# Two passes over half of the tokens, and Strassen's seven block products for gate and up

## The chip, the core and the metric

The program runs on one core of a Trainium2 chip. TensorE multiplies and writes PSUM; VectorE (DVE), ScalarE (ACT) and GpSimd (POOL) do the elementwise work; SyncE (SP) issues the DMAs. PEld is TensorE's weight load. The metric is the device time of one execution in microseconds (us). Before the change three runs took 1820.6, 1825.97 and 1830.25 us; the median is 1825.97.

## The reference

One layer of a decoder: input projection, sparse attention beside a state-space layer, output projection, then a feed-forward network (FFN). The change touches the FFN on 1024 prompt tokens and 32 sample tokens, with D_MODEL 1024 and D_FF 2816:

```python
x = x + gate1 * mix
h = rmsnorm(x, prm['norm_ffn_g']) * (1.0 + scale2) + shift2
f = (jax.nn.silu(h @ prm['w_ffn_gate']) * (h @ prm['w_ffn_up'])) @ prm['w_ffn_down']
return x + gate2 * f
```

All is float32. The kernel multiplies in TensorE's fp32r type: each operand is split into a high part (a cast on ACT) and a low part (a subtraction), and a product is three matmuls: high with high, high with low, low with high.

## The kernel before

The mix phase multiplies tiles of 128 tokens by the output projection (`mix_product`, tiles mx6, mx5, ...), adds the residual, and normalizes (`mix_norm`, tiles mn6, ...: eight transposes, then a modulation that leaves the token tile transposed and split in `h2h` and `h2l`, 1056 columns for 1024 prompt and 32 sample tokens). A string, `REST`, gives the order in which the program is written: `x6` is the product of tile 6, `n6` its norm, `f2` a third of the FFN's first step.

The FFN walks D_FF in 22 steps f of 128 columns. A step loads 512 KB each of gate, up and down weights, splits them (L409 cast on ACT, L410 subtraction on DVE), and multiplies gate and up with all tokens in three thirds of 352 columns (L1810: 2 weights x 8 row blocks x 3 matmuls a third, 144 a step). Silu (L1813), the product (L1816) and the split of the result (L1817 on ACT, L1818 on POOL) follow. Every second step, `down` multiplies two steps' results by the down weights: 8 token tiles x 2 halves x 6 matmuls of 512 columns (L1853, 96 a pair of steps), each group of six added to `acc` in SBUF by DVE (L1859). After the last step acc is scaled on POOL (L1843), the residual is added (L1844), and the last groups go out (L1862 to L1864).

A scheduler orders the instructions of each engine when the program is built, by estimates of their times; each engine then runs its own list in order. Tiles have a fixed number of buffers (`bufs`); a new tile waits until the one whose buffer it takes has been read.

Of the kernel before, what the change touches and what calls it, by code (L numbers as in the profile page):

```python
# [89 lines left out]
class Kernel:  # L90
# [1573 lines left out]
    def phase_mix(self):  # L1664
        for tt in self.MIX:
            self.mix_product(tt)
        h2 = self.open("h2", side="right")
        self.h2h = h2.tile([128, 8, 1056], F32R, name="h2h")
        self.h2l = h2.tile([128, 8, 1056], F32R, name="h2l")
        self.pw = self.open("pw", side="right")  # L1670
# [71 lines left out]
    def mix_norm(self, tt, xn):  # L1742
# [6 lines left out]
        if tt < 8:  # L1749
            self.modulated(xn, self.h2h[:, :, sl], self.h2l[:, :, sl], 2, 3, wo, nm, "xn", 2, self.ps_s(nm + "t"))  # L1750
        else:
            h = wo.tile([128, 8, 128], F32, tag="xn", name="h2s").rearrange("p k n -> p (k n)")[:, :256].rearrange("p (k n) -> p k n", k=8)
# [4 lines left out]

    def phase_ffn(self, first):
# [4 lines left out]
        acc = pe.tile([128, 8, 1024], F32, name="acc", bufs=1)  # L1763
        accs = pe.tile([128, 512], F32, name="accs", bufs=1)
        pend = []
        for f in range(NF):
            if f:
                first = self.ffn_weights(f, pe)
                for n in (2, 0, 1):
                    self.ffn_gate(f, n, *first)  # L1770
                first = first[1:]
            ah, al, as_ = first
            dn = pe.tile([128, 1024], F32, tag="wd", name=f"wd{f}", bufs=3)
            nc.sync.dma_start(dn, A["w_ffn_down"][0, 128 * f:128 * f + 128])
            dh = pe.tile([128, 1024], F32R, tag="dh", name=f"dh{f}")
            dl = pe.tile([128, 1024], F32R, tag="dl", name=f"dl{f}")
            self.split(dn, dh, dl)
            pend.append((dn, dh, dl, ah, al, as_))
            if len(pend) == 2:
                self.down(f, pend, acc, accs, pe)  # L1780
                pend = []
        self.close("pe", "pf", "pw", "h2", "pse")

    def ffn_weights(self, f, pe):

        nc, A, pf = self.nc, self.A, self.pf
        W = []
        for i, n in enumerate(("w_ffn_gate", "w_ffn_up")):
            raw = self.pw.tile([128, 8, 128], F32, tag="wr", name=f"wr{f}_{i}", bufs=2)
            nc.sync.dma_start(raw, A[n][0].rearrange("(k p) n -> p k n", p=128)[:, :, 128 * f:128 * f + 128])  # L1790
            wh, wl = ((pe if f % 2 else pf).tile([128, 8, 128], F32R, tag=f"w{f % 2}", name=f"w{x}{f}_{i}", bufs=4) for x in "hl")
            self.split(raw, wh, wl)
            W.append((wh, wl))
        ah, al = ((pe if f % 3 else pf).tile([128, 1024], F32R, tag="ahl", name=f"a{x}{f}", bufs=4 if f % 3 else 2) for x in "hl")
# [111 lines left out]
```

## Time and profile before

| | us |
|---|---|
| median of three runs | 1825.97 |
| lowest, highest | 1820.6, 1830.25 |
| the profiled execution | 1828.84 |
| its span, first to last instruction | 1827.1 |
| PE busy (94%) | 1709.1 |
| DVE busy (53%) | 972.2 |
| ACT busy (34%) | 618.9 |
| POOL busy (23%) | 427.1 |

The profile's time of one matmul runs from its start to its modelled end, and matmuls overlap, so the cost of one in a stream is the distance from one start to the next in the timeline. Busy shares of a stage come from a view by windows.

### The profile page before, as it was taken

The numbers are of one execution on the slowest core, as the hardware profiler recorded it, in microseconds if no ns is written. First come the engines' busy times: TensorE is split into PE (matmuls) and PEld (weight loads), VectorE is DVE, ScalarE is ACT, GpSimd is POOL, SyncE is SP. The second block draws the span as 40 slices with busy tenths as digits, with TensorE's granted clock in tenths as the row PEclk, the third lists the DMA queues.
The fourth block names the chain that finished last, engine by engine and source line by source line (L and its number), as shares of the span: only waits on it lengthen the run. The fifth ranks groups of instructions, "written<-read, shape, count | busy, mean of one in ns | idle before, by whom it ended". The sixth has DMA issues, their size and how long they took to land.

```text
span 1827.1 us, 29355 instructions
## 1 busy us (share of the span) xinstructions
PE 1709.1 (94%) x11546; PEld 1439.4 (79%) x11546; DVE 972.2 (53%) x2330; ACT 618.9 (34%) x1247; POOL 427.1 (23%) x817
## 2 busy tenths in 40 slices
PE   6998999899796899999989989999999999999997
PEld 3898988788564665655657888998998999999996
DVE  4867647588988466566535443323333333333346
ACT  4523146455453355565433341111111111211210
POOL 2344545232015313341122210110110110110150
PEclk9999999899898999999999999999999999999999
DMA  8333243645231345413114221101201201201113
GB/s 297 105 86 106 70 152 119 219 157 193 65 112 63 71 161 195 152 61 104 55 60 138 92 93 58 58 24 50 67 24 47 70 24 47 70 24 47 53 47 141
DMA packets 132699, 172.43 MB, mean 94 GB/s; under 512 B 17176, under 2 KB 92312, under 8 KB 132304
## 3 DMA queue, kind: packets, MB, share of 16 engines
q1 hardware_dynamic: 123024, 136.62, 23.4%
q0 software_dynamic: 9408, 33.89, 5.8%
q8 instruction: 91, 1.49, 0.3%
q14 instruction: 48, 0.39, 0.1%
q10 hardware_dynamic: 128, 0.04, 0.0%
HBM read 143.88 MB, written 25.46 MB: 93 GB/s over the span
## 4 chain that ended last, share of the span: by engine, by line
PE 61%; DVE 6%; DMA 4%; ACT 2%; issue 1%; POOL 1%; SPq 1%; DVEq 0%; ACTq 0%; POOLq 0%
PE gu L1810 19%; PE dn L1853 13%; PE g L1810 5%; PE u L1810 4%; PE aso L1283 3%; PE as L1205 1%; PE as L1206 1%; SPq L1596 1%; PE acs L1258 1%; PE mx8M L1728 1%; PE mx2M L1728 1%; PE mx5M L1728 1%; PE mx0M L1728 1%; PE mx1M L1728 1%; PE mx4M L1728 1%
## 5 line engine op out<-in xcount | busy, mean ns | idle before, releaser
L1810 PE MATMUL gu<-h2h,wh 128*128 128x352 f32 x704 | 227.8, 324 | 5.0 <-ACT h2h L870 5.0
L1810 PE MATMUL gu<-h2h,wl 128*128 128x352 f32 x704 | 227.3, 323 | 0.0
L1810 PE MATMUL gu<-h2l,wh 128*128 128x352 f32 x704 | 226.8, 322 | 0.0
L1859 DVE TENSOR_TENSOR acc<-acc,dn 128x512 f32<-128x512 f32 x144 | 98.9, 687 | 229.9 <-PE dn L1853 229.9
L1818 POOL TENSOR_TENSOR al<-fa,ah 128x352 fp32r<-128x352 f32 (+1 forms) x66 | 69.6, 1054 | 414.8 <-ACT ah L1817 408.8
L1813 ACT ACTIVATE fa<-gu 128x352 f32<-128x352 f32 x44 | 20.4, 465 | 412.1 <-PE gu L1810 412.1
L1853 PE MATMUL dn<-dh,ah 128*128 128x512 f32 x352 | 140.3, 399 | 5.6 <-DVE fin L1862 5.2
L1810 PEld LDWEIGHTS gu<-h2h,wh 128*128 128x128 f32 x704 | 132.5, 188 | 7.9 <-ACT h2h L870 5.3
L1853 PE MATMUL dn<-dl,ah 128*128 128x512 f32 x352 | 138.7, 394 | 0.0
L1853 PE MATMUL dn<-dh,al 128*128 128x512 f32 x352 | 138.3, 393 | 0.0
L1810 PEld LDWEIGHTS gu<-h2l,wh 128*128 128x128 f32 x704 | 133.0, 189 | 3.8
L1810 PEld LDWEIGHTS gu<-h2h,wl 128*128 128x128 f32 x704 | 132.7, 188 | 3.1
L1816 DVE TENSOR_TENSOR fa<-fa,gu 128x352 f32<-128x352 f32 x44 | 22.9, 521 | 143.0 <-ACT fa L1813 143.0
L409 ACT CAST wh<-wr 128x1024 fp32r<-128x1024 f32 x44 | 46.0, 1048 | 151.8 <-PE g L1810 77.0
L1205 PE MATMUL as<-kst,aqA 128*128 128x320 f32 (+4 forms) x192 | 76.7, 403 | 16.2 <-ACT ap L1222 9.3
L1853 PEld LDWEIGHTS dn<-dh,ah 128*128 128x128 f32 x352 | 66.1, 188 | 24.5 <-ACT wh L409 7.5
L410 DVE TENSOR_TENSOR wl<-wr,wh 128x1024 fp32r<-128x1024 f32 x44 | 58.8, 1339 | 49.3 <-ACT wh L409 49.3
L1853 PEld LDWEIGHTS dn<-dl,ah 128*128 128x128 f32 x352 | 66.1, 188 | 15.6
L1853 PEld LDWEIGHTS dn<-dh,al 128*128 128x128 f32 x352 | 66.3, 188 | 8.1
L1222 ACT ACTIVATE ap<-as,asm 128x640 f32<-128x640 f32 (+3 forms) x64 | 55.8, 873 | 46.6 <-DVE asm L1221 31.3
L1221 DVE TENSOR_REDUCE asm<-as 128x1 f32<-128x640 f32 (+3 forms) x64 | 58.5, 918 | 20.7 <-PE as L1209 19.8
L1206 PE MATMUL as<-kst,aqB 128*128 128x320 f32 (+4 forms) x192 | 65.1, 344 | 4.7 <-ACT aqB L1168 4.7
(2137 smaller groups left out, 4667.9 us busy)
## 6 DMA issues: line engine op xcount, KB each, us to landing
wada<-in_w_ada SPq DMA_DIRECT2D x24, 1024.0 KB
wr<-in_w_ffn_gate SPq DMA_DIRECT2D x22, 512.0 KB
wr<-in_w_ffn_up SPq DMA_DIRECT2D x22, 512.0 KB
wd<-in_w_ffn_down SPq DMA_DIRECT2D x22, 512.0 KB
bx<-in_x_prompt SPq DMA_DIRECT2D x8, 512.0 KB
s_raw<-in_cache_kv_win SPq DMA_DIRECT2D x8, 512.0 KB
wor<-in_w_out SPq DMA_DIRECT2D x16, 256.0 KB
ex<-x_d SPq DMA_DIRECT2D x8, 512.0 KB
```

Source lines behind the costliest of these rows:

```text
L409: self.nc.scalar.copy(hi, raw)
L410: self.nc.vector.tensor_tensor(lo, raw, hi.bitcast(F32), op=ALU.subtract)
L1205: nc.tensor.matmul(Sv, qA[:, h, :], kk, start=True, stop=False)
L1206: nc.tensor.matmul(Sv, qB[:, h, :], kk, start=False, stop=not mt)
L1221: nc.vector.tensor_reduce(mx[:, :1], Sv, axis=ax, op=ALU.max, negate=True)
L1222: nc.scalar.activation(Pv, Sv, AF.Exp, bias=mx[:, :1], accum_out=l[:, h:h + 1])
L1283: nc.tensor.matmul(O[64 * g:64 * g + 64, 256 * hf:256 * hf + 256], V[:n, 64 * g:64 * g + 64], pT[:, 256 * g:256 * g + 256], start=first, s ...
L1728: nc.tensor.matmul(M[:P, :], X[k][b], w[:, k, c], start=m == 0, stop=m == 23)
L1810: nc.tensor.matmul(gu[i], w[:, k, :], h[:, k, 352 * n:352 * n + 352], start=m == 0, stop=m == 23)
L1818: nc.gpsimd.tensor_tensor(al[:, cols], a[:, :w], ah[:, cols].bitcast(F32), op=ALU.subtract)
L1853: nc.tensor.matmul(p, a[:, sl], w[:, c], start=m == 0, stop=m == 5)
L1859: nc.vector.tensor_tensor(o, o, p, op=ALU.add)
```

## The change

The block matrix with gate and up as one axis and the two halves of the 1024 rows of h as the other is multiplied with a 2 x 2 arrangement of the activations (row half by token half). Instead of eight block products a step there are seven, of sums of blocks ("forms"), numbered 1, 5, 6, 2, 7, 4, 3 in the order in which they are written. For that the tokens are cut in two passes of 528 columns (PASS), each pass in two halves of 264. Each pass walks all 22 steps, so every weight is loaded, summed and split twice. A product is 4 row blocks x 3 matmuls of 264 columns; X, Z and Y are PSUM accumulators, and X is copied out three times on the way (fa), while the next product goes on adding to it. The seven forms of the activations (F1 to F7) are built once a pass: for the first in the mix phase (`F` in REST), for the second from a copy in DRAM (`h_d`, tiles hb). The FFN's first step no longer stands between the mix products.

```diff
@@ -1664,27 +1664,33 @@
     def phase_mix(self):
         for tt in self.MIX:
             self.mix_product(tt)
...
+        self.fm = self.open("fm", side="right")
+        self.h_d = self.scratch("h_d", (128, 16 * 264)).rearrange("p (a b k n) -> p a b k n", a=2, b=2, k=4)
+        self.hr = self.open("hr")
+        self.raw = self.hr.tile([128, 2, 2, 4, 264], F32, name="hraw")
         self.tags = "tt"
...
+            elif kind == "F":
+                self.ffn_forms(0, self.raw, self.hr)
+                self.close("hr")
+                self.pw = self.open("pw", side="right")
+                self.pf = self.open("pf", side="right")
+                self.hs = self.pf.tile([128, NF, 32], F32, name="hs")
+                first = self.ffn_weights(0)
...
-    REST = "x6 n8 x5 n7 x0 n6 x1 n5 n0 f2 n1 x4 x2 n2 x3 n4 f0 n3 f1"
+    PASS = ((7, 6, 0, 1), (5, 4, 2, 3))
+    REST = "x6 n8 x0 n7 x1 n6 n0 n1 F x5 x4 n5 n4 x2 n2 x3 n3"
...
+            for half in range(2):
+                for kh in range(2):
+                    nc.vector.tensor_copy(self.raw[:, kh, half, :, 256:], h[:, 4 * kh:4 * kh + 4, 8 * half:8 * half + 8])
+                    nc.sync.dma_start(self.h_d[:, kh, half, :, 256:], h[:, 4 * kh:4 * kh + 4, 16 + 8 * half:24 + 8 * half])
...
+        if ps:
+            for kh in range(2):
+                nc.sync.dma_start(self.h_d[:, kh, half, :, c], h[:, kh])
     def phase_ffn(self, first):
@@ -1760,119 +1785,187 @@
...
+        for ps in range(2):
+            acc = pe.tile([128, 4, 1024], F32, tag="acc", name=f"acc{ps}", bufs=1)
+            pend = []
+            if ps:
+                B = self.pe_blocks(pe)
+                self.ffn_forms(1, B, pe)
+            for f in range(NF):
+                if ps or f:
+                    first = self.ffn_gate(ps, f, self.ffn_weights2(self.ffn_weights(f), pe), pe)
+                ah, al = first
+                dn = pe.tile([128, 1024], F32, tag="wd", name=f"wd{ps}{f}")
+                nc.sync.dma_start(dn, A["w_ffn_down"][0, 128 * f:128 * f + 128])
+                dh = pe.tile([128, 1024], F32R, tag="dh", name=f"dh{ps}{f}")
+                dl = pe.tile([128, 1024], F32R, tag="dl", name=f"dl{ps}{f}")
+                nc.scalar.copy(dh, dn)
+                nc.gpsimd.tensor_tensor(dl, dn, dh.bitcast(F32), op=ALU.subtract)
+                pend.append((dn, dh, dl, ah, al))
+                if len(pend) == 2:
+                    self.down(ps, f, pend, acc, accs, g2, pe)
+                    pend = []
...
+    def pe_blocks(self, pe):
+        B = []
+        for kh in range(2):
+            for half in range(2):
+                b = self.pw.tile([128, 4, 264], F32, tag="wr", name=f"hb{kh}{half}", bufs=self.WR)
+                self.nc.sync.dma_start(b, self.h_d[:, kh, half])
+                B.append(b)
+        return [B[:2], B[2:]]
+    WR = 3
+    def ffn_forms(self, ps, B, pool):
+        nc = self.nc
+        if ps == 0:
+            B = [[B[:, kh, half] for half in range(2)] for kh in range(2)]
+        t = [pool.tile([128, 4, 264], F32, tag="ft", name=f"ft{ps}{i}", bufs=2) for i in range(3)]
+        self.F = {}
+        def put(n, b):
+            h, l = (self.fm.tile([128, 4, 264], F32R, tag=f"{n}{x}", name=f"F{ps}{n}{x}", bufs=1) for x in "hl")
+            nc.scalar.copy(h, b)
+            (nc.gpsimd if n in "23" else nc.vector).tensor_tensor(l, b, h.bitcast(F32), op=ALU.subtract)
+            self.F[n] = (h, l)
+        S = nc.vector.tensor_tensor
+        S(t[0], B[0][1], B[0][0], op=ALU.subtract)
+        put("1", B[0][0])
+        put("5", t[0])
+        S(t[1], B[1][1], t[0], op=ALU.subtract)
+        put("6", t[1])
+        put("2", B[1][0])
+        S(B[0][1], B[1][1], B[0][1], op=ALU.subtract)
+        put("7", B[0][1])
+        S(t[2], B[1][0], t[1], op=ALU.subtract)
+        put("4", t[2])
+        put("3", B[1][1])
+    def ffn_weights(self, f):
+        nc, A, pw, pf = self.nc, self.A, self.pw, self.pf
...
+        g, u = (pw.tile([128, 1056], F32, tag="wr", name=f"wr{nm}_{i}", bufs=self.WR)[:, :1024].rearrange("p (k n) -> p k n", k=8) for i in range(2))
+        for r, n in ((g, "w_ffn_gate"), (u, "w_ffn_up")):
+            nc.sync.dma_start(r, A[n][0].rearrange("(k p) n -> p k n", p=128)[:, :, 128 * f:128 * f + 128])
+        S = pw.tile([128, 4, 4, 128], F32, tag="ws", name=f"ws{nm}", bufs=1)
+        nc.vector.tensor_tensor(S[:, 0], u[:, :4], u[:, 4:], op=ALU.add)
+        nc.vector.tensor_tensor(S[:, 1], S[:, 0], g[:, :4], op=ALU.subtract)
+        nc.gpsimd.tensor_tensor(S[:, 2], g[:, :4], u[:, :4], op=ALU.subtract)
+        nc.gpsimd.tensor_tensor(S[:, 3], g[:, 4:], S[:, 1], op=ALU.subtract)
+        return self.ffn_split({}, (("1", g[:, :4]), ("5", S[:, 0]), ("6", S[:, 1])), pf), (("2", g[:, 4:]), ("7", S[:, 2]), ("4", u[:, 4:]), ("3", S[:, 3]))
+    def ffn_weights2(self, first, pe):
+        return self.ffn_split(*first, pe)
+    def ffn_split(self, W, what, pool):
+        nc = self.nc
+        for n, s in what:
+            h, l = (pool.tile([128, 4, 128], F32R, tag=f"w{n}{x}", name=f"w{n}{x}{self.nw}", bufs=1) for x in "hl")
+            nc.scalar.copy(h, s)
+            nc.vector.tensor_tensor(l, s, h.bitcast(F32), op=ALU.subtract)
+            W[n] = (h, l)
+        return W
+    def ffn_gate(self, ps, f, W, pe):
...
+        both = self.ps_s(f"gu{nm}")
+        X, Z, Y = both[:, 0, :264], both[:, 1, :264], self.ps_t(f"gy{nm}")[:, :264]
+        a = pe.tile([128, 3, 264], F32, tag="fa", name=f"fa{nm}", bufs=2)
+        c = pe.tile([128, 2, 264], F32, tag="fc", name=f"fc{nm}", bufs=2)
+        def product(out, n, start=False):
+            (wh, wl), (bh, bl) = W[n], self.F[n]
+            m = 0
+            for k in range(4):
+                for (w, b) in ((wh, bh), (wh, bl), (wl, bh)):
+                    nc.tensor.matmul(out, w[:, k, :], b[:, k, :], start=start and m == 0, stop=m == 11, skip_group_check=True)
+                    m += 1
+        product(X, "1", True)
+        nc.scalar.copy(a[:, 0], X)
+        product(Z, "5", True)
+        product(X, "6")
+        nc.scalar.copy(a[:, 1], X)
+        product(Y, "2", True)
+        nc.vector.tensor_tensor(c[:, 0], Y, a[:, 0], op=ALU.add)
+        product(X, "7")
+        nc.scalar.copy(a[:, 2], X)
+        nc.vector.tensor_tensor(a[:, 2], Z, a[:, 2], op=ALU.add)
+        product(X, "4")
+        product(Z, "3")
+        nc.vector.tensor_tensor(c[:, 1], Z, a[:, 1], op=ALU.add)
         for i in range(2):
-            m = 0
-            for k in range(8):
...
+            nc.scalar.activation(c[:, i], c[:, i], AF.Silu)
+        nc.vector.tensor_tensor(c[:, 0], c[:, 0], X, op=ALU.mult)
+        nc.vector.tensor_tensor(c[:, 1], c[:, 1], a[:, 2], op=ALU.mult)
+        ah, al = (pe.tile([128, 2, 256], F32R, tag=f"ah{x}", name=f"a{x}{nm}", bufs=4) for x in "hl")
+        for i in range(2):
+            nc.scalar.copy(ah[:, i], c[:, i, :256])
+        nc.gpsimd.tensor_tensor(al, c[:, :, :256], ah.bitcast(F32), op=ALU.subtract)
+        nc.gpsimd.tensor_copy(self.hs[:, f, 16 * ps:16 * ps + 16].rearrange("p (a n) -> p a n", a=2), c[:, :, 256:])
+        return ah, al
+    def down(self, ps, f, pend, acc, accs, g2, pe):
         nc = self.nc
         last = f == NF - 1
-        d = self.ada_d
-        p = self.ps_o(f"dns{f}")
-        for i, (dn, _, _, _, _, as_) in enumerate(pend):
+        if ps:
+            p = self.ps_o(f"dns{f}")
+            for i, (dn, _, _, _, _) in enumerate(pend):
+                for hf in range(2):
+                    q = 32 * (2 * i + hf)
+                    nc.tensor.matmul(p[q:q + 32, :], self.hs[:, f - 1 + i, :], dn[:, 512 * hf:512 * hf + 512], start=True, stop=True)
...
+        for i, tt in enumerate(self.PASS[ps]):
+            sl = slice(128 * tt, 128 * tt + 128)
+            if last:
+                x1 = pe.tile([128, 1024], F32, tag="ex", name=f"ex1_{tt}")
+                nc.sync.dma_start(x1, self.x1_d[sl])
+                nc.gpsimd.tensor_tensor(acc[:, i], acc[:, i], g2, op=ALU.mult)
+                nc.vector.tensor_tensor(acc[:, i], acc[:, i], x1, op=ALU.add)
             for hf in range(2):
-                q = 32 * (2 * i + hf)
-                nc.tensor.matmul(p[q:q + 32, :], as_, dn[:, 512 * hf:512 * hf + 512], start=True, stop=True)
...
+                p = self.ps_o(f"dn{ps}{f}{tt}{hf}")
...
-                        nc.tensor.matmul(p, a[:, sl], w[:, c], start=m == 0, stop=m == 5)
+                        nc.tensor.matmul(p, a[:, i // 2, 128 * (i % 2):128 * (i % 2) + 128], w[:, c], start=m == 0, stop=m == 5)
...
-                    t = fin[hf][:, tt % 2]
-                    nc.vector.tensor_tensor(t, p, g2[:, c], op=ALU.mult)
-                    nc.vector.tensor_tensor(t, t, o, op=ALU.add)
-                    nc.sync.dma_start(self.O[0][0, sl, c], t)
+                    nc.vector.tensor_tensor(p, p, g2[:, c], op=ALU.mult)
+                    nc.vector.tensor_tensor(o, o, p, op=ALU.add)
+                    nc.sync.dma_start(self.O[0][0, sl, c], o)
...
```

**PE, the end of the mix phase.** mx3M is the last mix product, that of tile 3; mn are the transposes of the norm, gu and gy the FFN's accumulators. Before:

```order
L1728 MATMUL mx3M_12723<-woh,mx3Xl_12691 128x512
L1728 MATMUL mx3M_12723<-wol,mx3Xh_12690 128x512
L862 MATMUL mn2t<-ident,mx2xc 128x128 x8
L862 MATMUL mn4t<-ident,mx4xc 128x128 x8
L1810 MATMUL gu_12791<-h2h,wh_0_12369 128x352
L862 MATMUL mn3t<-ident,mx3xc 128x128 x8
L1810 MATMUL gu_12791<-h2l,wh_0_12369 128x352
```

After:

```order
L1734 MATMUL mx3M_12727<-wol,mx3Xh_12694 128x512
L1734 MATMUL mx3M_12727<-woh,mx3Xh_12694 128x512
L1768 MATMUL mn2t<-ident,mx2xc 128x128 x8
L1734 MATMUL mx3M_12727<-woh,mx3Xl_12695 128x512
L1768 MATMUL mn3t<-ident,mx3xc 128x128 x8
L1893 MATMUL gu_12822<-F01h,w1h_12311 128x264
```

The transposes of tiles 2 and 4 no longer stand between tile 3's last matmul and its transposes; the FFN's first matmul comes behind them.

**DVE, one step of the first pass, after.** Names end in the step's number (w5l10: low part of weight form 5, step 10; fc09, fa09, gu09: pass 0, step 9; dn: a group of the down product).

```order
L1861 TENSOR_TENSOR ws10_14583<-wr10_1_14580 128x512
L1953 TENSOR_TENSOR acc0_12929<-acc0_12929,dn0710_14205 128x512
L1862 TENSOR_TENSOR ws10_14583<-ws10_14583,wr10_0_14579 128x512
L1875 TENSOR_TENSOR w5l10_14593<-ws10_14583,w5h10_14592 128x512
L1901 TENSOR_TENSOR fc010_14619<-gy010_14617,fa010_14618 128x264
L1875 TENSOR_TENSOR w7l10_14605<-ws10_14583,w7h10_14604 128x512
L1904 TENSOR_TENSOR fa09_14407<-gu09_14405,fa09_14407 128x264
L1875 TENSOR_TENSOR w4l10_14609<-wr10_1_14580,w4h10_14608 128x512
L1907 TENSOR_TENSOR fc09_14408<-gu09_14405,fa09_14407 128x264
L1910 TENSOR_TENSOR fc09_14408<-fc09_14408,gu09_14405 128x264
L1875 TENSOR_TENSOR w3l10_14613<-ws10_14583,w3h10_14612 128x512
L1911 TENSOR_TENSOR fc09_14408<-fc09_14408,fa09_14407 128x264
```

Rows of other steps' weights between these are left out. Before, a step's DVE list was two splits of 1024 columns, three products of 352, one split of the down weights and eight additions to acc.

**SP, the join of the two passes, after.** hb are the four blocks of the second pass's activations, in the three buffers of the weights' tag wr; wr22 are the weights of the second pass's first step; ex1 residuals of the first pass.

```order
L1859 DMA wr21_1_16517<-in_w_ffn_up 128x8x128
L1820 DMA hb00_16760<-h_d 128x1056
L1820 DMA hb01_16762<-h_d 128x1056
L1820 DMA hb10_16764<-h_d 128x1056
L1820 DMA hb11_16766<-h_d 128x1056
L1938 DMA ex1_1_16735<-x1_d 128x1024
L1859 DMA wr22_0_16803<-in_w_ffn_gate 128x8x128
L1859 DMA wr22_1_16804<-in_w_ffn_up 128x8x128
```

The fourth block takes the first block's buffer, and the next weights those of the second and third.

## Rows read from the trace of the kernel before

**Rows 1.** Windows view, 1144 to 1785: window, length, busy us (x instructions), clock, DMA.

```profile
1144.00:1785.00 641.00, 641.00 (x3623) 593.60 (x3623) 209.81 (x268) 102.66 (x164) 83.16 (x83) 1.00 0.15 46
```

**Rows 2.** Groups of matmuls: line, shapes, count | busy us, mean ns | idle before.

```profile
L1810 PE MATMUL gu<-h2h,wh 128*128 128x352 f32 x704 | 227.8, 324 | 5.0 <-ACT h2h L870 5.0
L1810 PE MATMUL g<-h2h,wh 128*128 128x352 f32 x176 | 56.8, 322 | 0.0
L1853 PE MATMUL dn<-dh,ah 128*128 128x512 f32 x352 | 140.3, 399 | 5.6 <-DVE fin L1862 5.2 <-DVE accs L1834 0.4
```

**Rows 3.** Timeline of PE, four stretches, first and last: start, duration, instruction.

```profile
1059.76 0.32 PE L1810 MATMUL gu<-h2l,wh 128*128 128x352 f32 x1
...
1065.85 0.32 PE L1810 MATMUL gu<-h2h,wh 128*128 128x352 f32 x1
...
174.81 0.28 PE L937 MATMUL q0p<-q0wh,hl 128*128 128x256 f32 x1
...
178.80 0.28 PE L937 MATMUL q0p<-q0wl,hh 128*128 128x256 f32 x1
...
151.88 0.29 PE L937 MATMUL kv2p<-kv2wh,hl 128*128 128x280 f32 x1
...
153.57 0.29 PE L937 MATMUL kv2p<-kv2wl,hh 128*128 128x280 f32 x1
...
1252.80 0.39 PE L1853 MATMUL dn<-dh,ah 128*128 128x512 f32 x1
...
1253.93 0.40 PE L1853 MATMUL dn<-dl,ah 128*128 128x512 f32 x1
```

**Rows 4.** Tile views: one operation's ns as min/median/max, first and last start.

```profile
L410 DVE TENSOR_TENSOR wl<-wr,wh x44: 1215/1226/1730, 963.7 to 1724.7; 128x1024 fp32r<-128x1024 f32 x44
L409 ACT CAST wh<-wr x44: 1039/1048/1054, 962.6 to 1722.9; 128x1024 fp32r<-128x1024 f32 x44
L1718 ACT CAST mx6Xh<-mx6xt x2: 586/586/587, 949.7 to 950.8; 128x512 fp32r<-128x512 f32 x2
L1859 DVE TENSOR_TENSOR acc<-acc,dn x144: 672/687/692, 1169.8 to 1773.7; 128x512 f32<-128x512 f32 x144
L1816 DVE TENSOR_TENSOR fa<-fa,gu x44: 507/521/523, 1011.9 to 1785.6; 128x352 f32<-128x352 f32 x44
```

**Rows 5.** Timelines of DVE and POOL where their instructions meet.

```profile
1759.29 2.40 POOL L1843 TENSOR_TENSOR acc<-acc,g 128x1024 f32<-128x1024 f32 x1 [2.51 <-DVE acc L1859]
...
1774.34 4.55 DVE L410 TENSOR_TENSOR dl<-wd,dh 128x1024 fp32r<-128x1024 f32 x2
1774.51 3.31 POOL L1843 TENSOR_TENSOR acc<-acc,g 128x1024 f32<-128x1024 f32 x1 [2.43 <-DVE acc L1859]
...
1167.87 0.95 POOL L1818 TENSOR_TENSOR al<-fa,ah 128x352 fp32r<-128x352 f32 x1 [6.37 <-ACT ah L1817]
1168.17 1.73 DVE L410 TENSOR_TENSOR wl<-wr,wh 128x1024 fp32r<-128x1024 f32 x1
```

**Rows 6.** Timeline of PE in the mix phase; brackets: idle before, and releaser.

```profile
964.81 0.50 PE L1728 MATMUL mx5M<-woh,mx5Xh 128*128 128x512 f32 x1 [2.18 <-ACT mx5Xh L1718]
...
1048.58 0.39 PE L1728 MATMUL mx3M<-wol,mx3Xh 128*128 128x512 f32 x1
...
1055.74 0.66 PE L1810 MATMUL gu<-h2h,wh 128*128 128x352 f32 x1 [5.02 <-ACT h2h L870]
1056.25 1.97 PE L862 MATMUL mn3t<-ident,mx3xc 128*128 128x128 f32 x8
```

**Rows 7.** Timeline of PE at the end.

```profile
1792.38 0.32 PE L1810 MATMUL u<-h2h,wl 128*128 128x352 f32 x1
...
1802.23 0.50 PE L1853 MATMUL dn<-dh,ah 128*128 128x512 f32 x1 [3.47 <-DVE fin L1862]
```

More of the change, by code (lines that the diff above doesn't have):

```diff
@@ L1666, in phase_mix @@
             self.mix_product(tt)
[L1667 to L1670, printed above, removed]
+        self.place = {tt: (p, i) for p, tiles in enumerate(self.PASS) for i, tt in enumerate(tiles)}
+        self.fm = self.open("fm", side="right")
+        self.h_d = self.scratch("h_d", (128, 16 * 264)).rearrange("p (a b k n) -> p a b k n", a=2, b=2, k=4)
+        self.hr = self.open("hr")
+        self.raw = self.hr.tile([128, 2, 2, 4, 264], F32, name="hraw")
         self.tags = "tt"
-        self.pf = self.open("pf", bufs=2, side="right")
-        ready, first = {}, None
-        for kind, tt in ((x[0], int(x[1:])) for x in self.REST.split()):
+        ready = {}
+        for x in self.REST.split():
+            kind, tt = x[0], int(x[1:] or 0)
             if kind == "x":
@@ L1762, in phase_ffn @@
         pe = self.open("pe", bufs=2)
-        acc = pe.tile([128, 8, 1024], F32, name="acc", bufs=1)
+        first = self.ffn_gate(0, 0, self.ffn_weights2(first, pe), pe)
         accs = pe.tile([128, 512], F32, name="accs", bufs=1)
[L1765 to L1794, printed above, removed]
-        as_ = pf.tile([128, 32], F32, tag="as", name=f"as{f}", bufs=3)
-        return W, ah, al, as_
@@ L1822, in down @@
-    def down(self, f, pend, acc, accs, pe):
+        g2 = pe.tile([128, 1024], F32, name="g2", bufs=1)
+        nc.sync.dma_start(g2, bass.AP(tensor=self.ada_d.tensor, offset=self.ada_d.offset + 3 * 1024, ap=[[0, 128], [1, 1024]]))
+        for ps in range(2):
[18 more added lines that the diff above has]
+                    pend = []
@@ new lines, in phase_ffn @@
+        self.close("pe", "pf", "pw", "fm", "pse")
+    def pe_blocks(self, pe):
[30 more added lines that the diff above has]
+        put("3", B[1][1])
@@ L1835, in down @@
-        if last:
-            self.finish_samples(accs, pe)
-            g2 = self.pw.tile([128, 1024], F32, tag="wr", name="g2", bufs=2)
-            nc.sync.dma_start(g2, bass.AP(tensor=d.tensor, offset=d.offset + 3 * 1024, ap=[[0, 128], [1, 1024]]))
-            fin = [pe.tile([128, 2, 512], F32, tag="ahl", name=f"fin{n}", bufs=4) for n in range(2)]
-            for tt in range(8):
-                x1 = (pe if tt % 2 else self.pf).tile([128, 1024], F32, tag=f"w{tt % 2}", name=f"ex1_{tt}", bufs=4)
-                nc.sync.dma_start(x1, self.x1_d[128 * tt:128 * tt + 128])
-                nc.gpsimd.tensor_tensor(acc[:, tt], acc[:, tt], g2, op=ALU.mult)
-                nc.vector.tensor_tensor(acc[:, tt], acc[:, tt], x1, op=ALU.add)
```

73 lines of the change are left out of this document (31 added, 42 removed).

## The prediction, on record before the changed kernel ran

> **What bounds the kernel now.** I read the windows first. From 1144 to 1785 us, most of the FFN, PE is busy in all of 641.00 us at full granted clock (1.00), while DVE has 209.81 us, ACT 102.66 and POOL 83.16 [rows 1]. In that stretch PE is the bound and nothing else comes near. Then the groups of matmuls: gate and up are three rows of 704 (gu) and six of 176 (g and u), 3168 matmuls of 352 columns; down is three of 352, 1056 matmuls of 512 columns (one row of each kind in [rows 2]). Their mean of some 322 ns isn't their cost, since they overlap. So last the timeline: from one start to the next.
>
> - 352 columns: 39 starts from 1059.76 to 1065.85, 6.09 / 38 = 0.1603 us.
> - 256 columns, same type and same size of weights: 35 starts from 174.81 to 178.80, 3.99 / 34 = 0.1174.
> - 280 columns: 14 starts from 151.88 to 153.57, 1.69 / 13 = 0.1300.
> - 512 columns: six starts from 1252.80 to 1253.93, 1.13 / 5 = 0.226 [rows 3].
>
> The cost goes by columns, with some 10 ns on top: 264 columns lie a third of the way from 256 to 280, 0.1174 + 8/24 x 0.0126 = 0.1216.
>
> **The change part by part.**
>
> *The products.* 7 products x 12 matmuls x 44 steps = 3696 of 264 columns, 3696 x 0.1216 = 449.4 us. Before: 3168 x 0.1603 = 507.8. PE gains 58.4 us, 11.5% and not the full eighth, since the 10 ns are paid 528 times more. Down keeps its 1056 matmuls and the mix its own. As PE is the bound, this is the whole gain; all else is what is lost again.
>
> *A step's work elsewhere.* A step of a pass now lasts 84 x 0.1216 + 24 x 0.226 = 15.6 us on PE. In it:
>
> - DVE, inputs both in SBUF: seven splits and two sums of 512 columns, half of 1.215 each, 0.61 x 9 = 5.5; one product of 264, some 0.3. Together 5.8.
> - DVE, one input in PSUM: four of 264 columns, between a half and the whole of 0.521, I take 0.42, and four additions to acc of 0.687: 1.7 + 2.75 = 4.4. DVE: 10.2 of 15.6.
> - ACT: seven casts of 0.586, one of 1.048, seven small ones at some 0.4: 7.9 [rows 4].
> - POOL: the down split of 1024 columns 2.40 (L1843's duration); three of 512, from 0.95 for 352 and 2.40 for 1024, 1.30 each; a copy of some 0.2: 6.5 [rows 5].
>
> No engine passes PE, but DVE and POOL don't run side by side. At 1774.34 two DVE splits took 4.55 us where two alone are 2.4, and POOL's scaling 3.31 where it takes 2.40 alone: POOL waited for the first split, the second for POOL. At 1167.87 POOL began, and the split begun at 1168.17 took 1.73 instead of 1.22 [rows 4, 5]. So 5.8 + 6.5 = 12.3 of 15.6 us of a step are serial.
>
> The Trainium skill (SBUF — State Buffer, Who interferes with whom) has this as an exclusive lock: a DVE instruction with two inputs in SBUF and a POOL instruction that reads SBUF wait for each other to the end. By that rule the split of 1168.17 had lasted 1.87 us (till 1168.82, then 1.22); the trace has 1.73, so it agrees within a tenth.
>
> What does PE lose by it? The order lets the work run one to two steps ahead: between product 7 and product 4 of a step, which must wait for ACT's copy of X, stand twelve or more matmuls of the next step, at least 1.4 us, in nearly all steps. Single weight buffers are free six or more us early in most places. The narrow place is X: fc09<-gu09 (the sum), then fc09 x gu09 on DVE have to end before product 1 two steps on, with some 1 to 2.5 us of PE work between. Four POOL operations a step, each in DVE's way two times of three for half its length, make DVE late by 0.67 x 0.5 x 6.5 = 2.2 us a step, but only what falls into the narrow place reaches PE. Bounds: 0 (before, PE had no wait in these 641 us) and one weight chain fully open a step, cast 0.59 + split 0.61 + 0.3 for the hand-overs, 1.5 us x 44 = 66. I take 0.4 us x 44 = 18, nearer to the zero that the trace shows, since PE's order has covers and DVE has a third of its time free.
>
> *End of the mix.* Before, from mx3M's end (1048.97) to mn3t's start (1056.25) 7.3 us pass, the norm's chain, with 5.0 us of PE idle; mn2t and mn4t stood in the gap [rows 6]. After, mn3t comes right behind the product and the FFN behind mn3t: idle 7.3, +2. The second product in PE's list waits for a split of weights queued on ACT and DVE behind tile 3's modulation: between nothing and another 7.3, I take +4. The first matmuls after a gap are slow (0.66 us at 1055.74 instead of 0.32), and more so after a longer one: +1. Tiles 0, 5 and 4 now have their transposes right ahead of their product, as mx5 alone had before, with 2.18 us idle [rows 6]: two more such gaps, +4. Sum 11, between 3 and 18 (the upper end since seven operations of forms come in one run on DVE there, 7 x 1.25 = 9 us).
>
> *The join of the passes.* From the first pass's last product 1 to the second's first product 3 PE has some 41 us of work. DVE adds nine operations of 1056 columns (1.25 each from 1.215 for 1024, 11.3), four residuals of 1.22, fourteen weight operations (8.5): with three products 25.6 us; POOL two forms (4.9), four scalings (9.6), two down splits, two al, four sums: 27. Serial 52.6 against 41: 12 us, some of which the next steps' free fifth takes over, and for which the load of wr22 behind hb01 makes up. Bounds 0 and 25.
>
> *The end.* Before, 34.7 us pass from the last up product (1792.4) to the end of the span, with 96 x 0.226 + 1.1 = 22.8 us of PE work in them; the rest is idle, 3.47 at one place [rows 7]. With 48 matmuls in the last down, half of the residuals and outputs remain: I take 8 idle instead of 12, -4 (-8 to +2).
>
> *Sum.* -58.4 + 18 + 11 + 12 - 4 = -21 us. The sum stands against the profiled execution: 1828.84 - 21 = 1807.4. The median of the runs lies 2.9 lower, so I say 1805.
>
> **The rivals.**
>
> *The covers hold.* If PE waits in the steps as little as before (0.1 us a step, 4) and the neighbours absorb the join (5): -58.4 + 4 + 9 + 5 - 4 = -44, 1782. For it: PE's unbroken 641 us, and the deep order. Against: DVE goes from a third to two thirds of the time, and the lock wasn't met often.
>
> *DVE and POOL set the pace.* The serial work makes evictions of X and the splits late in every step; DVE's list is in order, so a split that waits for POOL's 2.40 us holds the evictions behind it. At 1.4 us a step (62) with 15 at the join: -58.4 + 62 + 11 + 15 - 4 = +26, 1852, slower. It decides from (58.4 - 11 - 12 + 4) / 44 = 0.9 us a step on. For it: 12.3 of 15.6 us serial, single buffers. Against: DVE's own time plus 2.2 us of waiting is 12.4 of 15.6.
>
> *Weight loads are the bound.* PEld is busy 593.60 of 641 us with 3623 loads, one per 0.177 us [rows 1]; 528 more would cost 528 x 0.177 = 93 and the gain be gone, 1826 + 93 + 37 = 1956. Against it: at 256 columns a matmul with its own load of the same size starts every 0.1174 us [rows 3]. The Trainium skill (Perfetto Trace Analysis, Identifying the Most-Contended Engine) judges TensorE's nearness to its limit by the busy share of the weight loads; by that rule 93% would leave no room for more loads. The 256-column rows disagree.
>
> That the seventh product isn't saved is no rival: the order of the changed program has 84 matmuls a step.
>
> **How the numbers follow.** Chances: forecast 0.54, covers hold 0.20, DVE and POOL 0.23, weight loads 0.03. Under half a per cent (9 us) can't be told from no change here. The forecast spreads some 15 us to either side of 1805: 0.42 faster, 0.11 same, 0.01 slower. The covers case is all faster; the DVE case is 0.04 same and 0.19 slower. Sums: faster 0.62, same 0.15, slower 0.23. The range of 8 in 10 goes from 1774 (covers hold, with every loss near its lower bound) to 1850 (most of the DVE case); the forecast's own is 1788 to 1822.
>
> **What would show it.** In the changed profile: 264-column starts 0.1216 us apart (0.16 or more would bear out the weight loads); PE's idle time in the steps, some 18 us and released by DVE at gu (X), against 4 or 60; splits of 512 columns on DVE with a mean of 0.7 or more where the shortest is near 0.61; a gap of 7 us ahead of mn3t and of 4 behind it; some 12 us of PE idle where the second pass begins; and from the last product to the end some 19 us. I am wrong if the gain of the products isn't near 58 us, or if PE waits over 0.9 us a step.

## The result, and the profile after

The changed kernel takes 1885.7 us (median of 4, 1878.9 to 1892.2) where the kernel before took 1823.7 (1820.6 to 1830.3): ratio 1.034, interval 1.029 to 1.038. It is slower by some 60 us. I had said 1805, and 1850 as the upper end; the time lies outside the range and on the other side. The two profiled executions have spans of 1883.7 and 1827.1 us, so 56.6 us are to be explained.

First the matmuls themselves. This is PE's timeline of the changed kernel (start, duration, instruction), one run of gate and up products without a wait, first and last row of 20:

```profile
1639.74 0.28 PE L1893 MATMUL gu<-F14h,w4l 128*128 128x264 f32 x1
...
1642.04 0.28 PE L1893 MATMUL gu<-F16h,w6l 128*128 128x264 f32 x1
```

2.30 / 19 = 0.121 us from start to start; the median over all 3696 is 0.122, against 0.1216 forecast from [rows 3]. The gain of the products is there. So the loss is time in which PE waits, and the windows view says where (window, length, then busy us of PE, PEld, DVE, ACT and POOL with instructions, clock, DMA):

```profile
1058.00:1435.00 377.00, 348.31 (x2276) 321.55 (x2275) 300.07 (x374) 157.98 (x321) 157.24 (x104) 0.96 0.33 99
1435.00:1495.00 60.00, 44.84 (x260) 39.88 (x260) 59.04 (x65) 24.38 (x45) 37.53 (x19) 0.86 0.40 125
1495.00:1845.00 350.00, 341.95 (x2219) 298.62 (x2218) 272.52 (x368) 145.30 (x295) 154.45 (x101) 0.99 0.29 88
```

The three rows are the first pass, the join of the passes and the second pass. In [rows 1] PE had no idle time and a clock of 1.00 with DVE busy a third of the time; here DVE is busy for 80% of the first pass, 98% of the join and 78% of the second pass, PE waits in each, and the mean clock falls below 1.

For a sum I took from the trace, for each matmul, the time from its start to PE's next start, and subtracted the usual spacing (0.122 at 264 columns, 0.160 at 352, 0.230 at 512). What is left over is time lost, be it a wait or a stretch at the lower clock. The steps are those of both passes without the 60 us around the join:

| term | forecast, us | measured, us |
|---|---|---|
| products, 3696 x 0.122 - 3168 x 0.1603 | -58.4 | -56.9 |
| lost in the steps (67.2 after, 3.1 before) | +18 | +64 |
| samples' down matmuls (21 after, 10 before) | 0 | +11 |
| mix, up to the first product | +11 | +15 |
| join, 60 us around it | +12 | +22 |
| lost after the last product (22 after, 12 before) | -4 | +10 |
| ahead of the mix, where nothing was changed | 0 | -8 |
| sum | -21 | +57 |

The largest error by far is the loss in the steps. Its cause can be read from one step. Rows of the timelines of DVE, POOL and PE, in this order (in brackets idle time before, and its releaser):

```profile
1229.75 1.17 DVE L1875 TENSOR_TENSOR w6l<-ws,w6h 128x512 fp32r<-128x512 f32 x1
1230.84 2.88 DVE L1875 TENSOR_TENSOR w1l<-wr,w1h 128x512 fp32r<-128x512 f32 x1
1233.64 0.42 DVE L1901 TENSOR_TENSOR fc<-gy,fa 128x264 f32<-128x264 f32 x1
1233.99 0.67 DVE L1875 TENSOR_TENSOR w7l<-ws,w7h 128x512 fp32r<-128x512 f32 x1
1234.58 0.42 DVE L1904 TENSOR_TENSOR fa<-gu,fa 128x264 f32<-128x264 f32 x1
...
1228.71 1.66 POOL L1864 TENSOR_TENSOR ws<-wr,ws 128x512 f32<-128x512 f32 x1 [0.63 <-DVE ws L1862]
1230.33 2.84 POOL L1807 TENSOR_TENSOR dl<-wd,dh 128x1024 fp32r<-128x1024 f32 x1
...
1235.06 0.39 PE L1893 MATMUL gu<-F04h,w4h 128*128 128x264 f32 x1 [2.05 <-DVE fa L1904]
```

POOL's sum S3 (the row ws) runs till 1230.37; w6l, begun at 1229.75, ends only at 1230.92, 0.55 after it. Then POOL's dl, begun at 1230.33, gets its 2.4 us of work in, and w1l, whose work is 0.68, ends at 1233.72, again 0.55 after dl. Behind w1l in DVE's list stand two evictions of PSUM, fc and fa, and product 4 waits 2.05 us for the latter. Neither needs a result of POOL.

This is the longest kind of wait in the steps. The list of PE's waits from 1050 to the end begins so (total us, times, longest):

```profile
PE gu L1893 <- DVE fa L1904: 14.8, 7, 3.3
PE dn L1947 <- DVE acc L1953: 13.7, 7, 6.6
```

Six of the seven waits for fa, 11.5 us, are in the first pass. Over 18 steps of the first pass the groups of DVE are (out<-in, shapes, count | busy us, mean ns | idle before):

```profile
L1862 DVE TENSOR_TENSOR ws<-ws,wr 128x512 f32<-128x512 f32 x18 | 35.3, 1958 | 0.4
L1875 DVE TENSOR_TENSOR w1l<-wr,w1h 128x512 fp32r<-128x512 f32 x18 | 32.6, 1811 | 0.0
L1861 DVE TENSOR_TENSOR ws<-wr 128x512 f32<-128x512 f32 x18 | 29.7, 1653 | 0.0
L1875 DVE TENSOR_TENSOR w2l<-wr,w2h 128x512 fp32r<-128x512 f32 x18 | 22.6, 1256 | 0.2 <-ACT w2h L1874 0.2
...
L1875 DVE TENSOR_TENSOR w3l<-ws,w3h 128x512 fp32r<-128x512 f32 x18 | 12.3, 684 | 0.0
...
L1904 DVE TENSOR_TENSOR fa<-gu,fa 128x264 f32<-128x264 f32 x18 | 7.6, 422 | 0.0
L1953 DVE TENSOR_TENSOR acc<-acc,dn 128x512 f32<-128x512 f32 x64 | 43.2, 680 | 27.8 <-PE dn L1947 27.4
```

Operations of one size take from 684 to 1958 ns where both inputs lie in SBUF, while those with an input in PSUM (fa, acc) keep their time: L1953 has 680 ns as acc had 687 in [rows 4]. The nine operations of a step that I had put at 5.5 us take 10.6.

A wait costs a second time. The windows around the same wait:

```profile
1231.00:1236.00 5.00, 2.95 (x22) 2.66 (x22) 4.00 (x4) 0.42 (x1) 2.17 (x1) 1.00 0.67 210
1237.00:1239.50 2.50, 2.50 (x13) 2.50 (x12) 0.69 (x1) 0.44 (x2) 0.00 (x0) 0.50 0.10 22
```

and PE's timeline in the second of them:

```profile
1237.10 0.42 PE L1893 MATMUL gu<-F03h,w3l 128*128 128x264 f32 x1
...
1237.76 0.42 PE L1893 MATMUL gu<-F03h,w3l 128*128 128x264 f32 x1
```

After the 2.05 us without work, and 1.4 us more of matmuls at the full clock, the granted clock is at its lower level, 0.50 (1.2 GHz), from 1236.5 to 1240.0, and a matmul of 264 columns comes every 0.22 us (0.66 / 3) instead of 0.122. In the first pass some 12 of the 50 us lost are such stretches.

### The profile page after: what moved, and what is told of

It reads as the page before. It is cut to its first block, busy times and chain, and to the rows that moved or that the text cites. A ratio compares the mean times of both kernels' runs of the same rounds, so it can differ in the third digit from the quotient of the medians.

```text
span 1883.7 us, 32056 instructions
## 1 busy us (share of the span) xinstructions
PE 1703.4 (90%) x12074; PEld 1408.0 (75%) x12074; DVE 1359.4 (72%) x2827; ACT 824.0 (44%) x1714; POOL 703.9 (37%) x953
## 5 line engine op out<-in xcount | busy, mean ns | idle before, releaser
L1863 POOL TENSOR_TENSOR ws<-wr,wr 128x512 f32<-128x512 f32 x44 | 63.2, 1436 | 338.3 <-DVE w3l L1875 330.9
L1953 DVE TENSOR_TENSOR acc<-acc,dn 128x512 f32<-128x512 f32 x144 | 97.5, 680 | 66.3 <-PE dn L1947 65.6
L1807 POOL TENSOR_TENSOR dl<-wd,dh 128x1024 fp32r<-128x1024 f32 x44 | 116.3, 2659 | 57.9 <-ACT dh L1806 38.6
L1909 ACT ACTIVATE fc<-fc 128x264 f32<-128x264 f32 x88 | 37.4, 425 | 103.0 <-DVE fc L1901 79.1
L1864 POOL TENSOR_TENSOR ws<-wr,ws 128x512 f32<-128x512 f32 x44 | 71.1, 1616 | 28.2 <-DVE ws L1862 27.6
L1875 DVE TENSOR_TENSOR w4l<-wr,w4h 128x512 fp32r<-128x512 f32 x44 | 41.3, 938 | 52.2 <-ACT w4h L1874 52.1
L1862 DVE TENSOR_TENSOR ws<-ws,wr 128x512 f32<-128x512 f32 x44 | 72.2, 1641 | 0.8
L404 POOL DMA_INDIRECT craw<-in_cache_kv_cmp,idx x32 | 35.0, 1094 | 99.1 <-ACT cxr L487 89.1
L1861 DVE TENSOR_TENSOR ws<-wr 128x512 f32<-128x512 f32 x44 | 67.9, 1543 | 5.3 <-DMA wr<-in_w_ffn_up 5.3
L404 POOL DMA_INDIRECT s_raw<-in_cache_kv_slc,idx x32 | 30.9, 967 | 93.3 <-PE s120o L850 44.7
L499 DVE TENSOR_TENSOR cXl<-ct,cXh 128x512 fp32r<-128x512 f32 x72 | 48.7, 684 | 15.2 <-ACT cXh L498 14.8
```

The costliest lines, as they stand in the source:

```text
L404: self.nc.gpsimd.indirect_dma_start(out=out, out_offset=None, in_=v, in_offset=bass.IndirectOffsetOnAxis(ap=self.idx[:, b, j:j + 1], axis=0))
L1807: nc.gpsimd.tensor_tensor(dl, dn, dh.bitcast(F32), op=ALU.subtract)
L1861: nc.vector.tensor_tensor(S[:, 0], u[:, :4], u[:, 4:], op=ALU.add)
L1862: nc.vector.tensor_tensor(S[:, 1], S[:, 0], g[:, :4], op=ALU.subtract)
L1863: nc.gpsimd.tensor_tensor(S[:, 2], g[:, :4], u[:, :4], op=ALU.subtract)
L1864: nc.gpsimd.tensor_tensor(S[:, 3], g[:, 4:], S[:, 1], op=ALU.subtract)
```

## The experiments

The theory: POOL's operations on SBUF and DVE's with two inputs in SBUF exclude each other; that, and not the length of DVE's list or the single weight buffers, makes evictions and splits late. The chips that ran them differ a little, so each is told as a ratio to the kernel before on the same chip (the changed kernel: 1.034; 0.01 is some 18 us). "Lost" is the excess described above.

**POOL's four subtractions left out.**

```diff
-                nc.gpsimd.tensor_tensor(dl, dn, dh.bitcast(F32), op=ALU.subtract)
-                pend.append((dn, dh, dl, ah, al))
+                pend.append((dn, dh, dh, ah, ah))
...
-        nc.gpsimd.tensor_tensor(S[:, 2], g[:, :4], u[:, :4], op=ALU.subtract)
-        nc.gpsimd.tensor_tensor(S[:, 3], g[:, 4:], S[:, 1], op=ALU.subtract)
...
-        nc.gpsimd.tensor_tensor(al, c[:, :, :256], ah.bitcast(F32), op=ALU.subtract)
```

The splits of forms 7 and 3 read `S[:, 0]` and `S[:, 1]` in place of the two sums left out.

> Left out, so part of the computation is missing: POOL's four subtractions of a step (weight sums S2 and S3, the low parts of the down weights and of the activations); the matmuls read the high part or another sum in their place, so that PE, ACT and DVE have the same instructions as in the changed kernel. Theory (POOL's operations stretch DVE's with two SBUF inputs, so evictions and splits reach PE late): splits of 512 on DVE go back to a mean near 0.68 us from 1.0, PE's lost time in the 44 steps falls from 64 us to under 15, the join from 22 to some 12: 1885 - 50 - 10 = 1825, between 1810 and 1840. Rival A (single weight buffers: casts and splits wait for the last reader and then come in a bunch): their waits stay, at most 15 us go: 1870 or more. Rival B (DVE's list is long by itself): DVE's own 10.2 us of a 15.6 us step remain, with little effect: 1860 or more.

1831.3 us, ratio 1.000 (0.998 to 1.001), some 62 us faster than the changed kernel. In the windows of the two passes PE now has next to no idle time:

```profile
1068.00:1400.00 332.00, 330.75 (x2286) 310.36 (x2287) 219.41 (x378) 164.91 (x324) 15.92 (x23) 0.99 0.37 114
1400.00:1460.00 60.00, 48.84 (x302) 43.82 (x300) 53.20 (x74) 27.19 (x50) 13.20 (x7) 0.89 0.45 145
1460.00:1790.00 330.00, 329.98 (x2178) 289.69 (x2177) 201.90 (x357) 140.90 (x287) 16.73 (x23) 1.00 0.29 88
```

DVE has the same instructions and is busy 66% and 61% instead of 80% and 78%. Lost in the steps: 6 us instead of 67. The single weight buffers are all still there, so they cost next to nothing by themselves: rival A falls. What goes with POOL's work is nearly the whole loss of the steps, though this run can't say whether because POOL kept DVE waiting or because POOL's results came late. At the join less goes than I expected, from 22 us to 16.

**The same work on DVE.** The four subtractions, and the two forms that POOL split, with `nc.vector` for `nc.gpsimd`; nothing is left out.

> The same four subtractions of a step, and the two low parts of forms that POOL made, on DVE instead; nothing is left out. DVE's own work in a step grows by 1.22 + 1.22 + 0.68 = 3.1 us to some 13.5, but no instruction of it meets a POOL instruction with SBUF inputs. Theory of the shared port: DVE's busy time in a step falls from 15.4 us (of 17.8) to 13.5, PE's lost time in the steps from 64 us to some 30: 1850, between 1830 and 1868, faster than the changed kernel. Rival B (the length of DVE's own list decides): 3.1 us more a step on the engine that is late: 1895 or more. Rival A (single buffers): within 10 us of 1885.

1846.3 us, ratio 1.007 (1.005 to 1.009): 49 us faster than the changed kernel with 3 us more of work a step on DVE. Two groups of DVE:

```profile
L1807 DVE TENSOR_TENSOR dl<-wd,dh 128x1024 fp32r<-128x1024 f32 x20 | 23.6, 1219 | 3.1 <-ACT dh L1806 3.1
...
L1875 DVE TENSOR_TENSOR w1l<-wr,w1h 128x512 fp32r<-128x512 f32 x21 | 14.3, 683 | 0.6 <-ACT w1h L1874 0.5
```

All operations of 512 columns are back at 680 to 687 ns. Lost in the steps: 19 us. A longer list without meetings beats a shorter one with them: rival B falls as the main cause. The longer list isn't free: 13 us more are lost in the steps than in the run without the work.

**POOL's work again, for nobody.** The version with all of it on DVE, and in each step:

```diff
+                sc = pe.tile([128, 1024], F32, tag="ex", name=f"du{ps}{f}")
+                nc.gpsimd.tensor_tensor(sc, dn, dh.bitcast(F32), op=ALU.subtract)
+                for i in range(3):
+                    nc.gpsimd.tensor_tensor(sc[:, :512], dn[:, :512], dh.bitcast(F32)[:, 512:], op=ALU.subtract)
```

> All the step's subtractions stay on DVE, as in the run with POOL's work on DVE (1846 us), and POOL gets work of the same kind again, one subtraction of 1024 columns and three of 512 a step with both inputs in SBUF, into a buffer that nobody reads. Nothing waits for POOL's results, only for the two tiles of down weights that it reads. Theory of the shared port: DVE's splits are stretched again, to a mean of 0.9 us or more from 0.68, DVE's list is now some 3 us a step longer than in the changed kernel, PE loses at least as much as in it: 1890 or more. Rival (in the changed kernel what counted was that POOL's results came late, not that POOL kept DVE waiting): within 10 us of 1846.

2012.6 us, ratio 1.101 (1.097 to 1.105): some 170 us more than without this work. Timelines of DVE and POOL:

```profile
1213.28 2.60 DVE L1879 TENSOR_TENSOR w2l<-wr,w2h 128x512 fp32r<-128x512 f32 x1
1215.80 3.40 DVE L1807 TENSOR_TENSOR dl<-wd,dh 128x1024 fp32r<-128x1024 f32 x1
1219.13 1.76 DVE L1868 TENSOR_TENSOR ws<-wr,ws 128x512 f32<-128x512 f32 x1
1220.81 2.28 DVE L1807 TENSOR_TENSOR dl<-wd,dh 128x1024 fp32r<-128x1024 f32 x1
1223.01 1.74 DVE L1879 TENSOR_TENSOR w7l<-ws,w7h 128x512 fp32r<-128x512 f32 x1
1224.68 0.42 DVE L1908 TENSOR_TENSOR fa<-gu,fa 128x264 f32<-128x264 f32 x1
...
1212.94 5.18 POOL L1809 TENSOR_TENSOR du<-wd,dh 128x1024 f32<-128x1024 f32 x2 [3.13 <-ACT dh L1806]
1218.08 11.18 POOL L1811 TENSOR_TENSOR du<-wd,dh 128x512 f32<-128x512 f32 x6
```

The two engines take turns: w2l has 2.60 us, since it ends 0.55 after the POOL operation of 1024 columns that began ahead of it (1212.94 to 1215.33). The next four likewise end 0.55 (512 columns) or 1.08 (1024 columns) after the POOL operation that they met, while fa, with its input in PSUM, keeps its 0.42. No instruction of DVE or PE waits for POOL's results in the first pass here, and PE's longest waits are for DVE's (36 us in the first pass for fa alone). So POOL's work beside DVE's is enough, whoever needs its results. The Trainium skill (SBUF — State Buffer, Who interferes with whom) describes an exclusive lock, in which the instruction that comes second waits until the first has ended; these rows agree with it. The work was bunched more closely than in the changed kernel, so the size of the loss doesn't carry over to it.

**Only the weight sums on DVE.** The first two of the four lines moved.

> Of POOL's four subtractions of a step only the two weight sums S2 and S3 go to DVE; the low parts of the down weights and of the activations stay on POOL. Theory: POOL's work with SBUF inputs falls from 6.5 to some 3.9 us a step, DVE's waiting for it from 4.6 to some 2.8, its own work grows by 1.4: 15.0 us a step against 15.4, and against 13.5 with all four moved. Of the 49 us that moving all four gained, some 15 to 25: 1865, between 1855 and 1880 (before at 1832). Rival (it is the 1024-column operation alone that reaches PE): within 8 us of 1894, the changed kernel's time on this scale.

1873.8 us, ratio 1.027 (1.023 to 1.031), between the two ends; the gain of some 12 us is smaller than the 15 to 25 that I expected (its interval reaches from some 0 to 25). Operations of DVE still meet POOL's dl and al: the sums L1864 and L1862, both on DVE here, have means of 1.34 and 1.18 us instead of 0.68. Lost in the steps: 50 us instead of 67.

**The samples' down matmuls together.**

```diff
-        nc.gpsimd.tensor_copy(self.hs[:, f, 16 * ps:16 * ps + 16].rearrange("p (a n) -> p a n", a=2), c[:, :, 256:])
+        ht = self.ht if f % 2 else self.pf.tile([128, 2, 16], F32, tag="ht", name=f"ht{nm}", bufs=2)
+        self.ht = ht
+        nc.scalar.copy(ht[:, f % 2].rearrange("p (a n) -> p a n", a=2), c[:, :, 256:])
+        if f % 2:
+            nc.scalar.copy(self.hs[:, f - 1:f + 1, 16 * ps:16 * ps + 16], ht)
```

> The samples' activations of two steps are copied together (by ACT instead of POOL), so that the four matmuls of the samples' down product come in one run of PE instead of two apart. Theory: a run lasts 1.0 us whether it has two or four of these matmuls, so 11 runs less take 11 us away, and POOL's 44 copies of 0.65 us that stand in DVE's way another 3: 1871, between 1864 and 1877. Rival: the runs fill time in which PE waits anyway, 1882 or more.

1883.2 us, ratio 1.028 (1.026 to 1.030), about 10 us less than the changed kernel's 1.034. (The 1871 was counted from the first chip's 1885; on this one the kernel before is 9 us slower.) The two intervals overlap, so the time alone doesn't settle it. The lists do. One run of these matmuls before, and one in the changed kernel (tile views: ns as min/median/max, first and last start; each matmul has two records):

```profile
L1830 PE MATMUL dns<-wd,as x8: 592/604/617, 1166.4 to 1166.9; 128*32 128x512 f32 x8
```

```profile
L1927 PE MATMUL dns<-wd,hs x4: 592/604/617, 1646.3 to 1646.8; 128*32 128x512 f32 x4
```

Four matmuls came in the time that now two take. They write separate strips of 32 PSUM partitions and run side by side, and a run lasts 1.0 us either way; the scheduler had put the two steps' pairs apart. With them together the time of these matmuls, over the whole kernel, went from 22.8 to 11.0 us. The loss in the steps stays at 66 to 67 us, so the 3 us that I expected from POOL's copies aren't seen.

**The join without its forms.** `pe_blocks` and `ffn_forms(1)` taken out.

> Left out: the second pass's forms; it multiplies by the first pass's (the output of four tiles is wrong by that). So the join has no loads, differences, casts and splits of forms; all else is the changed kernel. Theory: the 22 us that PE loses between 1435 and 1495 us fall to the loss of an ordinary stretch of 60 us, some 7, so 15 us go: 1870, between 1863 and 1876. Rival: what PE loses there is late weights that the next steps catch up anyway, and the loss comes back in the second pass: 1882 or more.

1887.2 us, ratio 1.029 (1.027 to 1.031), some 8 us less, half of what I expected, with intervals that overlap (1870 and 1882 were counted from 1885, too). At the join 11.9 us are lost instead of 22, and in the second pass 19 instead of 17, so little of it comes back there. By this accounting the forms are half of the join's loss; the time alone doesn't show it. With POOL's work on DVE as well (a single run, its time not compared):

> Left out: the second pass's forms, as in the run that used the first pass's twice; and POOL's subtractions are on DVE. In the 60 us around the join PE lost 21.7 us in the changed kernel, 11.9 without the forms, 14.9 with POOL's work on DVE. Theory: forms and shared port are the two causes of the join's loss, so with both gone under 6 us are left of it. Rival (a third cause, the residuals and the new acc tile, which the next pass's first down product has to wait for): 8 us or more are left.

7 to 8.5 us are left, by where the 60 us are placed against the second pass's first product; I expected under 6, the rival 8 or more. The 14.9 of the expectation likewise becomes 18.7 when the window is placed as in the changed kernel. Forms and shared port together explain some two thirds of the join's loss, and the rest isn't settled.

**Versions meant to be faster.** The first has POOL's work on DVE, the samples' matmuls together, tile 2's norm after tile 3's product (`x3 n2 n3`), and buffers of their own for the samples' last rows:

```diff
...
-        x1 = pe.tile([128, 1024], F32, tag="ex", name="ex1_8")[:32]
+        x1 = pe.tile([128, 4, 264], F32, tag="ft", name="ex1_8", bufs=2).rearrange("p k n -> p (k n)")[:32, :1024]
...
```

> A version meant to be faster, nothing left out: POOL's subtractions on DVE, the samples' four matmuls in one run, the samples' last loads in buffers of their own, so that the residuals' loads needn't wait for them, and tile 2's transposes placed into the gap ahead of tile 3's. From 1846: -10 (runs of the samples' matmuls, as measured), -9 (the wait of 9.0 us at the end, since the four loads then come some 15 us earlier), -2 (mix): 1825, between 1816 and 1834, with before at 1832. Rival: DVE, which has 80% of its time taken, is late elsewhere instead: 1840 or more.

1818.8 us, ratio 0.996 (0.993 to 0.998): a little faster than before. What the last edit does is seen on SP's queue, in the first of the residuals' loads of the version with POOL's work on DVE, and of this one:

```profile
1820.82 0.33 SPq L1938 DMA_DIRECT2D ex<-x_d  x1
```

```profile
1776.75 5.39 SPq L1942 DMA_DIRECT2D ex<-x_d  x2
```

They were issued from 10.8 us after the last product (1810.0) on, as the samples' rows held the two buffers, and now from 9.6 ahead of it (1786.3) on; lost at the end are 18.3 us instead of 25.8, the new longest wait being the samples' matmuls for their copies (6.4). The second version leaves tile 2 in its place and moves tile 3's norm behind the first step's products:

```diff
-            elif kind == "n":
+            elif kind == "n" and tt != 3:
...
         first = self.ffn_gate(0, 0, self.ffn_weights2(first, pe), pe)
+        self.mix_norm(3, self.x3)
...
```

The lines left out let tile 3's norm use buffers and PSUM banks of the FFN, and keep the first version's other edits.

> As the version with all three edits, but in place of tile 2's transposes it is the last norm (tile 3, which only the second pass needs) that moves: its transposes come after the first step's gate and up products in the program, so that PE needn't wait for the chain product, norm, transpose (8.0 us) and for the PSUM banks behind it (4.3 us) ahead of the first product. Theory: the first product starts right behind the last product of the mix but for the forms and weights that it needs: -8 to -12 against the other version: 1815, between 1806 and 1825 (before at 1832). Rival: the first product then waits for the weights' splits instead, at most -3.

1812.6 us, ratio 0.991 (0.988 to 0.994), the fastest. From tile 8's mix product to the FFN's first product 208.3 us pass, against 221.3 in the first version (and 219.7 in the changed kernel, so tile 2's other place alone had gained nothing). But PE's list has the transposes only twelve matmuls on, and they still make it wait (the window ends ahead of the eighth):

```profile
1058.67 1.73 PE L1769 MATMUL mn3t<-ident,mx3xc 128*128 128x128 f32 x7 [5.02 <-DVE mx3xc L1744]
```

A third version was to take that wait and that of the samples' matmuls away.

> The fastest version so far (1812.6 with before at 1826.7, ratio 0.991) with two orders changed, nothing left out: the samples' last down product comes after two tiles of the last down product instead of ahead of them, since it waited 6.1 us for the copied activations there, and tile 3's norm comes after the second step's gate and up products in the program, not after the first's (its transposes made PE wait 5.0 us). Theory: each wait lies on the path, both go: -6 and -4, ratio 0.986, between 0.982 and 0.990. Rival: tile 3's transposes are put at the same place of PE's list by the scheduler, and the samples' last operations on DVE come last instead: no change, 0.990 to 0.993.

1825.7 us, ratio 0.994 (0.992 to 0.996): no gain over the second. The rival's account held: the scheduler put the transposes in the same place (wait 5.0), and the samples' operations on DVE now stood among the last tiles' (a wait of 2.9 for acc; the longest of the end, 3.5, is for al).

## Why the prediction was wrong

- **The products** were right: 0.122 against 0.1216, and -56.9 against -58.4. The rival of the weight loads is refuted by the same spacing.
- **The step that failed is "what does PE lose by it"**, 0.4 us a step, 18 in all. It measured 1.5 us a step, 64 more than before: the rival "DVE and POOL set the pace" (1.4 a step, 62 us, 1852), which I had named and given 0.23. That DVE and POOL exclude each other, read from [rows 5], was right; what it costs PE went wrong at three places.
  - *DVE's waiting.* I counted each POOL operation as in DVE's way two times of three for half its length, 2.2 us a step. The nine operations of a step with two inputs in SBUF take 10.6 us in the first pass, and 9 x 0.68 = 6.1 alone: 4.5 us of waiting, two thirds of POOL's 6.5 instead of one third. Operations that stand one behind the other in DVE's list can pay the whole of dl, not half (2.88 for w1l). I also took too little for 512 columns, 0.61 from half of 1024, where it is 0.68.
  - *The narrow place.* I looked for it at X, where fc has to be done before product 1 two steps on. No wait of product 1 for fc is in the list of the steps. PE waits at product 4, which I had waiting for ACT's copy of X alone: it never starts before DVE's fa behind that copy has ended, and in nine of the 44 steps it starts within 0.06 us of that end. (This fa reads Z and product 4 adds to X; both are halves of one tile, gu. Whether the program needs that wait no run shows.)
  - *What reaches PE.* I set it near zero because PE had no wait in [rows 1] and DVE had a third of its time free. I had put PE's covers at 1.4 us or more; a single meeting with dl costs 2.2, and the evictions of PSUM, which POOL doesn't stretch, stand behind it in the same list. An average share says nothing of that.
- **The price of the lower clock** I left out: some 12 us in the first pass, some 20 in all steps and the join.
- **The samples' matmuls** I put at no cost, since their number was unchanged; +11 us by their place.
- **The end of the mix**: +15 measured, in my bounds of 3 to 18; the gaps that I named are there, 7.45 us ahead of mn3t and 3.86 behind it.
- **The join**: +22, near the upper bound of 25. DVE has 59 of its 60 us busy there; about half of the loss are the forms, by the accounting above.
- **The end**: I forecast -4 and lost 10. The longer waits come from residual rows that were loaded late, since the samples' two rows held the buffers of tag `ex` from the join on; I had not read that tag's users. In the changed kernel this is argued from the order of the loads; moving them was tried in the first version above, together with other edits.
- The part ahead of the mix, which the change doesn't touch, was 8 us shorter in this execution; over the twelve profiled kernels it is between 838 and 854 us.

Not settled by a run: why the first pass loses 50 us and the second 17 with the same instructions a step. DVE's nine operations wait 4.5 us a step in the first pass and 3.7 in the second, so that alone isn't it. The trace suggests the place in the list: in the first pass dl meets w1l, close ahead of the evictions fc and fa (mean 1.81 us), and four of the six waits of product 4 come 4.2 us after the start of a w1l of 2.87 or more; in the second pass w1l has a mean of 0.68, and there is one such wait. Both losses go when POOL's work goes.

## What to carry to other kernels

Before counting an engine's free time, add up what it shares: where two lists of DVE and POOL both work on SBUF, take the sum of their times as one list (here 10.2 + 6.5 = 16.7 us by the forecast's own prices, for a step of 15.6), and charge the longest POOL operation whole to whatever stands behind it. Moving work from a free engine onto a busier one can be the faster choice: here 3 us more a step on DVE gained 49 us. Where a change halves the cover of PE, look at the longest single delay of the engine that releases it, not at its share of busy time.

## What was not expected of the hardware

- POOL's copy of 16 columns (hs) takes 0.20 us when it meets nothing and 0.65 in the changed kernel's steps: it waits its turn like the large ones.
- A gap of 2.05 us on PE in a stretch of matmuls at the full clock was followed by a stretch at half the clock, and that came late: the gap ends at 1235.06, the stretch begins at 1236.5. The first pass of the changed kernel has seven such stretches, the kernel before none between 1060 and 1785.
- Two or four of the samples' matmuls that write separate strips of PSUM partitions take the same 1.0 us.
